# Two fp32 up projections between the spread and the dense stage, and the last 72 row fetches behind the scaling of zb

## The chip, the cores and the metric

One core of a Trainium2 chip runs the whole kernel. The metric is the device time of one execution in microseconds (us). The kernel before took 2037.93 us, the median of three runs (2034.81 to 2039.86). Engines are named as in the profile: PE (TensorE), DVE (VectorE), ACT (ScalarE), POOL (GpSimd) and SP (SyncE, which here only issues DMAs).

## The reference, cut to what matters

Two transformer blocks act on 512 tokens of width 1024, in float32. What the change touches is the end of the first block, a mixture of 16384 single-neuron experts, and the second block.

```python
# first block, per block of 128 tokens: 8 heads, 16 experts each, 128 in all per token
q = (xb @ wq).reshape(t, 8, 2, 128)
...                                   # two top-16 lists per head, joined to 16 experts
e = i1 * 128 + i2
g = softmax(c_top)
ue, ve = u[e], v[e]
act = gelu(einsum('thkd,td->thk', ue, xb))
x = x + einsum('thk,thkd->td', g * act, ve)
x = rmsnorm(x, final_norm_g)
# second block
h = rms_norm(x, g2)
q, k, v, qi, ki, wi, z_a, u_b, z_b, gates = split(h @ w_in_2)
a = dsa_attention(q, k, v, qi, ki, wi, 128) * silu(z_a)
b = multiscale_pool(u_b) * pool_scale * silu(z_b)
y = g0 * (a @ w_branch_a) + g1 * (b @ w_branch_b)
x = x + y @ w_out
```

## The kernel before, in words

The tokens form four tiles of 128, numbered 0 to 3. The experts are evaluated in two ways at once.

**Tiles 0 and 3 gather** (`gather`, L529). For each of the 128 experts k of a token, `fetch` (L552) has POOL issue an indirect DMA that brings one row of `peer_u` per token into a `rows` tile (128 x 1024, four buffers), and DVE multiplies and sums it with the token (L539). A second pass of 128 fetches brings rows of `peer_v`, and DVE adds each, scaled, to the accumulator `gx` (L546). So a tile needs 256 fetches, and each needs DVE before its buffer is free again. Constants `HOLDS = [168, 0]` say from which fetch on a tile waits for a mark, which is a small POOL copy near the end of the spread (`hold`, L610). All fetches of tile 3 wait for it.

**Tiles 1 and 2 are dense** (`first`, from L1016; `dense`, L620). All 16384 experts are computed for 256 tokens, in 128 groups e of 128 experts. An up projection `up(e)` (L595) loads 512 KB of `peer_u`, transposes it on PE (8 transposes), copies it out with ACT, multiplies it with the tokens, and applies Gelu. In the fp32 form (`xw` as the only operand) that is 16 matmul instructions and ACT copies; in the split form (`dh`, a high and a low fp32r half) it is 24, and DVE computes the low half of every transposed piece. Groups 0 to 36 (`EARLY`) and nine more (`WX`, kept in the pool `gb`) go through the fp32 form ahead of the dense loop. The **spread** (L559) writes the gates of all experts into `sa` and `sb` for four tokens at a time. After it, L1062 multiplies the nine kept results into `sb`, the pool `gb` is given up, `dh` is made from `xw` in its place (ACT, then DVE: L1065, by `split`, L129), and the **dense loop** starts: for each e a product with 512 KB of `peer_v` on PE (L646, half of the groups in three fp32r passes, the other half in fp32), and in between the up projections of groups 46 to 127 in the split form (L657).

**The second block** (`second`, L741) runs over the groups of tiles [0, 1, 2] and then [3]. For each group: add what the first block left (`after`, L661), two norms, transposes to `hl`, projections for qi/k/v, the index scores with 16 rounds of top-8 on DVE (`index`), projections for q, z_a, u_b and z_b (scaled on POOL at L821), attention (`attend`), the gates, the pooled branch, and two rounds of output projections. For three tiles every weight is split in two: ACT makes the high half, POOL the low one (L129, `wlo`). Tile 3 can't start before its last row has been added, and its `hl` lies in the buffer that the first group's last projection reads.

The program gives the order of the calls; a scheduler that simulates a timeline then fixes one order of instructions per engine, in which a later call can be moved ahead where its inputs are ready sooner. An engine works through its own list strictly in that order. `issue_after(mark)` keeps an instruction behind the marked one. The tile-3 gather is called at L1010, before the second block.

```python
for t, hold in zip(GATHER, HOLDS):
    n.gather(t, hold)
n.second_setup(b2)
for ts in GROUPS:
    n.second(ts, bp, bw)
```

Of the kernel before, what the change touches and what calls it, by code (L numbers as in the profile page):

```python
# [14 lines left out]
AF = mybir.ActivationFunctionType  # L15
OP = mybir.AluOpType
# [50 lines left out]
class Net:  # L67
# [197 lines left out]
    def mixer(self, ts):  # L265
# [17 lines left out]
        with tc.tile_pool(name="mq", bufs=1) as mq, tc.tile_pool(name="mw", bufs=2) as mw:  # L283
# [19 lines left out]
            def front(i, t, h):  # L303
                w_ = (t + 1) * P
                pe = []
                sm = mw.tile([P, 2], F32, name="sm", bufs=DEEP + 2)
                for p in range(2):
# [3 lines left out]
                    pe.append(self.expo(mw, s[:, :w_], self.abias[:, T - w_:T], w_, sm[:, p:p + 1], f"p{p}", slopes[h], P0B - p))  # L311
                r = mw.tile([P, 3], F32, name="rc", bufs=DEEP + 2)
                nc.vector.reciprocal(r[:, 0:2], sm)
# [214 lines left out]

    def gather(self, t, hold):  # L529

        nc, a = self.nc, self.a
        ei, gw = self.ei[t], self.gw[t]
        act = self.act[t]
        pause = self.normed if t == 0 else None
        xn = self.ga.tile([P, D], F32, name="gx", bufs=1)
        nc.sync.dma_start(xn, self.xnd[t])
        for k in range(P):
            r = self.fetch(a["peer_u"][0], ei, k, self.mark if k >= hold else pause if k >= PAUSE else None)
            nc.vector.scalar_tensor_tensor(r, r, 1.0, xn, op0=OP.mult, op1=OP.mult, accum_out=act[:, k:k + 1])  # L539
        nc.scalar.activation(act, act, AF.Gelu)  # L540
        nc.vector.tensor_tensor(act, act, gw, OP.mult)
        x = self.ga.tile([P, D], F32, name="gx", bufs=1)
        nc.sync.dma_start(x, self.xd[t])
        for k in range(P):
            r = self.fetch(a["peer_v"][0], ei, k, self.mark if P + k >= hold else pause)
            nc.vector.scalar_tensor_tensor(x, r, act[:, k:k + 1], x, op0=OP.mult, op1=OP.add)  # L546
        if t == GATHER[-1]:
            self.xs = {t: x}
        else:
            nc.sync.dma_start(self.xd[t], x)  # L550
# [44 lines left out]
    def up(self, e, hl, nt, dst, pool, half, bank=None):  # L595

        nc = self.nc
        u = self.st.tile([P, D], F32, name="raw", bufs=RAW)
        nc.sync.dma_start(u, self.a["peer_u"][0, e * P:(e + 1) * P, :])
        h = self.sc()  # L600
        for f in range(2):
            uT = [pool.tile([P, 4, P], x.dtype, name="uT", bufs=half) for x in hl]
            self.tsplit(uT, u[:, f * 512:(f + 1) * 512], 0, 0, bank)
            for k in range(4):
                ps = self.passes([x[:, k, :] for x in uT], [x[:, 4 * f + k, 0:nt] for x in hl])
                for q, (x, y) in enumerate(ps):
                    nc.tensor.matmul(h[:, :nt], x, y, start=f == k == q == 0, stop=f == 1 and k == 3 and q == len(ps) - 1)  # L607
        nc.scalar.activation(dst, h[:, :nt], AF.Gelu)  # L608

    def hold(self, gb):  # L610

        t = gb.tile([P, 1], F32, name="held")
        self.mark = self.nc.gpsimd.tensor_copy(t, self.sb_last).ins

    def early(self, e, hl, nt, wp, bufs, pool, half):
        w = wp.tile([P, nt], F32, name="w", bufs=bufs)
# [3 lines left out]
    def dense(self, ts, hl, sa, sb, dn, ue):  # L620

        nc, a = self.nc, self.a
        n = len(ts)
        nt = n * P
        mm = nc.tensor.matmul
        slot = lambda e: sa[:, e, :] if e < EARLY else sb[:, e - EARLY, :]

        V = {}

        def vp(e):  # L630
            V[e] = dn.tile([P, D], F32, name="v", bufs=VB)
            nc.sync.dma_start(V[e], a["peer_v"][0, e * P:(e + 1) * P, :])

        def op(e):
            v, w = [V.pop(e)], [slot(e)]
            if e % MIX[1] < MIX[0]:
                for x in (v, w):
                    hl_ = [dn.tile(list(x[0].shape), F32R, name=f"h{x[0].shape[1]}", bufs=1),
                           dn.tile(list(x[0].shape), F32R, name=f"l{x[0].shape[1]}", bufs=1)]
                    self.split(*hl_, x[0])  # L640
                    x[:] = hl_
            for i in range(n):
                for c in range(2):
                    ps = self.passes([x[:, i * P:(i + 1) * P] for x in w], [x[:, c * 512:(c + 1) * 512] for x in v])
                    for q, (x, y) in enumerate(ps):
                        mm(o[i][c], x, y, start=e == q == 0, stop=e == P - 1 and q == len(ps) - 1)  # L646

        o = [[self.acc() for _ in range(2)] for _ in range(n)]
        for e in range(VB - 1):
            vp(e)  # L650
        done = first = EARLY + WX
        for e in range(P):
            if e + VB - 1 < P:
                vp(e + VB - 1)
            op(e)
            while done < P and done - first < (e + 1) * (P - first) / LASTUP:
                nc.vector.tensor_tensor(slot(done), slot(done), self.early(done, hl, nt, dn, 1, ue, HALFE), OP.mult)  # L657
                done += 1
        self.sums = dict(zip(ts, o))
# [81 lines left out]
    def second(self, ts, bp, bw):  # L741

        nc, a = self.nc, self.a
        w = a["w_in_2"][0]
        n = len(ts)
        t0 = ts[0]
        ncol = n * P
        hl = self.pair(n)
        g_fin, g_2 = self.gains
        G = bp.tile([P, n, 2 * D], F32, name="G", padded_shape=[P, GN, 2 * D])  # L750
        for i, t in enumerate(ts):
            x = self.after(t)
            h = G[:, i, 0:D] if i else self.hn.tile([P, D], F32, name="h2", bufs=1)
# [9 lines left out]
        zb = bp.tile([P, n, 512], F32, name="zb", padded_shape=[P, GN, 512])  # L763
# [54 lines left out]

        def put_zb(i, p):
            nc.scalar.activation(zb[:, i, :], p, AF.Silu)  # L820
            nc.gpsimd.tensor_tensor(zb[:, i, :], zb[:, i, :], self.psc, OP.mult)  # L821

        self.proj(hl, w, 1064, 512, 8, n, put_za)
        nc.vector.tensor_copy(uT[:, :, 0:16], self.tail)
# [2 lines left out]
        self.proj(hl, w, 2088, 512, 8, n, put_zb)  # L827
        av = qk[:, :, 0:512]
        self.attend(ts, qT, bm, av, bw)
        for b in range(4):  # L830
            mb = self.row(bw, a["merge_bias_2"][0, b // 2, (b % 2) * 512:], 512, "once", bufs=OB, padded_shape=[P, 640])

            def put_g(i, p):
                d = G[:, i, b * 512:(b + 1) * 512]
                nc.vector.tensor_tensor(d, p, mb, OP.add)
                nc.scalar.activation(d, d, AF.Sigmoid)
            self.proj(hl, w, 2600 + b * 512, 512, 8, n, put_g)

        hl = self.pair(n)
# [25 lines left out]
        hl = self.pair(n)  # L865
# [101 lines left out]
RAW = 3  # L967
HALFE = 4
WX = 9
DEEP = 1  # L970
PEB = 2
P0B = 2
VB = 2
EARLY = 37
# [11 lines left out]
GATHER = [0, 3]  # L986
# [12 lines left out]
def build(tc, a, const_at, dbg=None):  # L999
    with ExitStack() as ctx:  # L1000
        n = Net(tc, ctx, a, const_at, dbg)
        pool = lambda name, bufs=1, **k: tc.tile_pool(name=name, bufs=bufs, **k)
        n.ga = ctx.enter_context(pool("ga", 2, side="right"))
        n.room(0, ctx.enter_context(pool("g0", side="right")))
        first(n, pool, ctx)
        n.tpn, n.nraw, n.whole, n.lone, n.lo_of = GN, 3, WHOLE, False, LO3
        with pool("tp2") as n.tp, pool("hn2", 2) as n.hn, pool("ws2") as n.ws, pool("b2") as b2, \
                pool("bp") as bp, pool("bw", 2) as bw:
            for t, hold in zip(GATHER, HOLDS):
                n.gather(t, hold)  # L1010
            n.second_setup(b2)
            for ts in GROUPS:
                n.second(ts, bp, bw)


def first(n, pool, ctx):  # L1016
    n.tpn, n.nraw = 3, 4
    n.whole, n.lone = WHOLE0, True
    nd = len(DENSE) * P
    with ExitStack() as right:  # L1020
# [27 lines left out]
        with pool("ue") as ue, pool("sa") as sap:  # L1048
            sa = sap.tile([P, EARLY, nd], F32, name="sa")
            for e in range(EARLY):  # L1050
                n.up(e, [n.xw], nd, sa[:, e, :], ue, HALFE, n.wide if e % 2 else None)
            for t in DENSE + [3]:
                n.select(t, se, idx, SP3 if t == 3 else 1)
            keys.close()
            with pool("sb") as sbp:
                sb = sbp.tile([P, P - EARLY, nd], F32, name="sb")
                with pool("gb", 2) as gb:
                    with n.tc.issue_after(n.picked):
                        ahead = [n.early(EARLY + i, [n.xw], nd, gb, WX, ue, HALFE) for i in range(WX)]
                    n.spread(idx, sa, sb, gb)  # L1060
                    for i, w in enumerate(ahead):
                        n.nc.vector.tensor_tensor(sb[:, i, :], sb[:, i, :], w, OP.mult)  # L1062
                with pool("dx") as dx:
                    dh = [dx.tile([P, 8, nd], F32R, name=f"dh{i}") for i in range(2)]
                    n.split(*dh, n.xw)  # L1065
                    picks.close()
                    with pool("dn", 2) as dn:
                        n.dense(DENSE, dh, sa, sb, dn, ue)
# [26 lines left out]
```

## Time and profile before

| what | us |
|---|---|
| median of three runs | 2037.93 (2034.81 to 2039.86) |
| the profiled execution | 2031.25 |
| its span in the profile | 2029.5 |
| PE busy | 1837.0 (91%) |
| DVE busy | 1515.5 (75%) |
| POOL busy | 859.6 (42%) |
| ACT busy | 741.0 (37%) |

The span is what the profiler sees of the execution, from the first instruction to the last; the 1.75 us that the profiled execution is longer lie around it. The shares are means over stages that have quite different limits, so they say little about a change in one place: at which time which engine idles, and for whom, is in the rows below.

### The profile page before, as it was taken

What the parts mean: (1) busy time and instruction counts of PE and PEld (TensorE: products, weight loads), DVE (VectorE), ACT (ScalarE), POOL (GpSimd) and SP (SyncE); (2) the same over time, 40 slices, a digit from 0 to 9 for tenths busy, and PEclk for the clock granted to TensorE, in tenths of its full rate; (3) what the DMA queues carried; (4) which work ended last, traced back from release to release, by engine and by line L of the source; (5) the groups of instructions that cost most, each with busy time, mean ns of one, the idle gap of its engine ahead of it and who ended that gap; (6) DMA issues with size and microseconds to landing.
All of it is one profiled execution on the core that took longest, in us unless ns stands there. A gap on an engine that the chain in (4) does not pass through costs nothing.

```text
span 2029.5 us, 27663 instructions
## 1 busy us (share of the span) xinstructions
PE 1837.0 (91%) x9646; PEld 1453.2 (72%) x9646; DVE 1515.5 (75%) x3064; ACT 741.0 (37%) x1504; POOL 859.6 (42%) x627
## 2 busy tenths in 40 slices
PE   7898988699989976999999999999976987889998
PEld 6597767699878965777877777777755765667644
DVE  1188998889995598877767777777878899974261
ACT  2243552333533784323232223232323333453231
POOL 0015566654344003454333444444448876654100
PEclk9999998799999998999999999999998897889999
DMA  9857998987566204999999999999988665762872
GB/s 342 280 167 255 314 323 290 326 293 252 175 208 236 88 22 179 358 353 344 367 328 343 347 356 345 345 352 336 359 275 301 220 192 177 234 200 80 304 258 83
DMA packets 182012, 538.23 MB, mean 265 GB/s; under 512 B 18032, under 2 KB 25328, under 8 KB 181744
## 3 DMA queue, kind: packets, MB, share of 16 engines
q1 hardware_dynamic: 108144, 268.00, 38.0%
q0 software_dynamic: 73728, 268.47, 37.2%
q8 instruction: 76, 1.25, 0.2%
q14 instruction: 64, 0.52, 0.1%
HBM read 528.53 MB, written 7.86 MB: 264 GB/s over the span
## 4 chain that ended last, share of the span: by engine, by line
PE 47%; DVE 18%; DMA 11%; issue 8%; POOL 3%; ACT 3%; SPq 0%; POOLq 0%; DVEq 0%; ACTq 0%
PE acc L646 17%; PE sc L607 13%; PE acc L205 9%; DMA rows<-in_peer_u,ei 4%; DMA rows<-in_peer_v,ei 4%; PE tr L154 4%; DVE gx L546 3%; POOL rows L555 3%; DVE rows L539 2%; ACT A L578 1%; DMA v<-in_peer_v 1%; PE acc L233 1%; DVE ix L406 1%; PE sc L927 1%; PE tr L936 1%
## 5 line engine op out<-in xcount | busy, mean ns | idle before, releaser
L555 POOL DMA_INDIRECT rows<-in_peer_u,ei x256 | 323.8, 1265 | 334.7 <-DVE rows L539 242.3
L555 POOL DMA_INDIRECT rows<-in_peer_v,ei x256 | 316.2, 1235 | 349.6 <-DVE gx L546 274.8
L546 DVE SCALAR_TENSOR_TENSOR gx<-rows,act,gx 128x1024 f32<-128x1024 f32 x256 | 384.5, 1502 | 47.9 <-DMA rows<-in_peer_v,ei 41.8
L539 DVE SCALAR_TENSOR_TENSOR rows<-rows,gx 128x1024 f32<-128x1024 f32 x256 | 310.8, 1231 | 37.8 <-DMA rows<-in_peer_u,ei 37.2
L607 PE MATMUL sc<-dh,uT 128*128 128x256 f32 x1968 | 296.4, 297 | 18.4 <-ACT dh L128 6.1
L607 PEld LDWEIGHTS sc<-dh,uT 128*128 128x128 f32 x1968 | 258.8, 191 | 54.0 <-issue 21.0
L205 PE MATMUL acc<-whi,Thi 128*128 128x512 f32 (+1 forms) x500 | 194.6, 427 | 25.5 <-ACT whi L128 17.8
L205 PE MATMUL acc<-wlo,Thi 128*128 128x512 f32 (+1 forms) x504 | 206.1, 428 | 9.7 <-POOL wlo L129 8.5
L607 PE MATMUL sc<-xw,uT 128*128 128x256 f32 x736 | 173.6, 387 | 14.4 <-ACT uT L157 14.3
L129 POOL TENSOR_TENSOR wlo<-raw,whi 128x1024 fp32r<-128x1024 f32 (+1 forms) x62 | 148.4, 2402 | 76.4 <-ACT whi L128 75.8
L205 PE MATMUL acc<-whi,Tlo 128*128 128x512 f32 (+1 forms) x432 | 171.4, 400 | 1.9 <-DVE Tlo L129 1.9
L646 PE MATMUL acc<-v,sb 128*128 128x512 f32 x368 | 165.7, 593 | 2.5 <-DMA v<-in_peer_v 2.4
L128 ACT ACTIVATE whi<-raw 128x1024 fp32r<-128x1024 f32 (+1 forms) x108 | 110.7, 1028 | 149.7 <-PE acc L205 67.8
L607 PEld LDWEIGHTS sc<-xw,uT 128*128 128x128 f32 x736 | 137.9, 194 | 32.8 <-ACT uT L157 15.8
L205 PEld LDWEIGHTS acc<-whi,Thi 128*128 128x128 f32 x500 | 97.7, 198 | 64.3 <-ACT whi L128 20.8
L129 DVE TENSOR_TENSOR uT<-tr,uT 128x512 fp32r<-128x512 f32 x164 | 109.0, 687 | 32.1 <-ACT uT L128 31.4
L205 PEld LDWEIGHTS acc<-wlo,Thi 128*128 128x128 f32 x504 | 100.4, 200 | 44.9 <-issue 15.6
L154 PE MATMUL tr<-c_ident,raw 128*128 128x128 f32 x880 | 130.6, 273 | 0.0
L128 ACT ACTIVATE uT<-tr 128x512 fp32r<-128x512 f32 x164 | 92.5, 595 | 81.1 <-PE tr L154 76.6
L608 ACT ACTIVATE w<-sc 128x256 f32<-128x256 f32 x91 | 34.8, 382 | 225.4 <-PE sc L607 220.6
L646 PEld LDWEIGHTS acc<-v,sb 128*128 128x128 f32 x368 | 66.4, 190 | 69.2 <-issue 66.1
L154 PEld LDWEIGHTS tr<-c_ident,raw 128*128 128x128 f32 x880 | 104.4, 141 | 10.9 <-issue 4.2
(332 smaller groups left out, 3362.6 us busy)
## 6 DMA issues: line engine op xcount, KB each, us to landing
raw<-in_peer_u SPq DMA_DIRECT2D x128, 512.0 KB, 6.4
v<-in_peer_v SPq DMA_DIRECT2D x128, 512.0 KB, 6.0
raw<-in_w_in SPq DMA_DIRECT2D x79, 512.0 KB, 4.7
raw<-in_w_out SPq DMA_DIRECT2D x22, 512.0 KB, 5.2
whi<-in_w_in SPq DMA_DIRECT2D x21, 512.0 KB, 6.5
raw<-in_peer_wq SPq DMA_DIRECT2D x21, 512.0 KB, 6.0
wlo<-in_w_in SPq DMA_DIRECT2D x20, 512.0 KB, 7.2
rows<-in_peer_u,ei POOLq DMA_INDIRECT x256, 6.9
```

The costliest lines, as they stand in the source:

```text
L128: self.nc.scalar.activation(hi, src, AF.Copy)
L129: (eng or self.nc.vector).tensor_tensor(lo, src, hi.bitcast(F32), OP.subtract)
L154: nc.tensor.transpose(p[:, c, :], src[:, (j + c) * P:(j + c + 1) * P], self.ident)
L205: self.nc.tensor.matmul(ps[i][:, :n], x, y, start=k == 0 and q == 0, stop=k == nk - 1 and q == len(ws) - 1)
L233: nc.tensor.matmul(ps[c][:, :ncol], x, y, start=k == 0 and q == 0, stop=k == 7 and q == len(ws) - 1)
L406: nc.vector.max_index(ix[:, r], v[:, r], src)
L539: nc.vector.scalar_tensor_tensor(r, r, 1.0, xn, op0=OP.mult, op1=OP.mult, accum_out=act[:, k:k + 1])
L546: nc.vector.scalar_tensor_tensor(x, r, act[:, k:k + 1], x, op0=OP.mult, op1=OP.add)
L555: self.nc.gpsimd.indirect_dma_start(out=r, out_offset=None, in_=src, in_offset=bass.IndirectOffsetOnAxis(ap=ei[:, k:k + 1], axis=0))
L607: nc.tensor.matmul(h[:, :nt], x, y, start=f == k == q == 0, stop=f == 1 and k == 3 and q == len(ps) - 1)
L608: nc.scalar.activation(dst, h[:, :nt], AF.Gelu)
L646: mm(o[i][c], x, y, start=e == q == 0, stop=e == P - 1 and q == len(ps) - 1)
```

## The change

The loop that starts the gathers now only runs each generator to its first `yield`. For tile 0 there is none and everything is issued as before. For tile 3 the generator stops ahead of fetch 56 of the `peer_v` pass; `second` resumes it after `attend` of the first group, and the 72 fetches left then wait for `scaled`, POOL's last multiplication of `zb` in that group, in place of the mark of the spread. Apart from that, groups 46 and 47 leave the dense loop: `link` computes their up projections in the fp32 form between the spread and the split of `xw`, leaves Gelu's result in PSUM, and DVE multiplies it into `sb` from there.

```diff
     def gather(self, t, hold):
...
         for k in range(P):
+            if t == GATHER[-1] and k == REST:
+                self.xs = {}
+                yield
+                hold, self.mark = 0, self.scaled
             r = self.fetch(a["peer_v"][0], ei, k, self.mark if P + k >= hold else pause)
...
-        nc.scalar.activation(dst, h[:, :nt], AF.Gelu)
+        h = h[:, :nt]
+        nc.scalar.activation(h if dst is None else dst, h, AF.Gelu)
+        return h
...
+    def link(self, e, hl, nt, dst, pool, half):
+
+        h = self.up(e, hl, nt, None, pool, half)
+        self.nc.vector.tensor_tensor(dst, dst, h, OP.mult)
...
-        done = first = EARLY + WX
+        done = first = EARLY + WX + LINK
...
-            nc.gpsimd.tensor_tensor(zb[:, i, :], zb[:, i, :], self.psc, OP.mult)
+            self.scaled = nc.gpsimd.tensor_tensor(zb[:, i, :], zb[:, i, :], self.psc, OP.mult).ins
...
         self.attend(ts, qT, bm, av, bw)
+        next(self.rest, None)
...
+LINK = 2
+REST = 56
...
-                n.gather(t, hold)
+                n.rest = n.gather(t, hold)
+                next(n.rest, None)
...
+                for e in range(EARLY + WX, EARLY + WX + LINK):
+                    n.link(e, [n.xw], nd, sb[:, e - EARLY, :], ue, HALFE)
                 with pool("dx") as dx:
```

## Rows read from the trace of the kernel before

**Rows 1.** The page, part 2: busy tenths in 40 slices of 50.7 us.

```profile
PE   7898988699989976999999999999976987889998
DVE  1188998889995598877767777777878899974261
```

**Rows 2.** Windows: stretch, length, busy time (instructions) per engine, clock, DMA share, GB/s.

```profile
710.00:780.00 70.00, 54.43 (x397) 47.23 (x395) 70.00 (x177) 63.00 (x199) 0.00 (x0) 1.00 0.05 16
780.00:793.00 13.00, 1.40 (x6) 0.93 (x5) 9.55 (x16) 2.33 (x2) 7.77 (x7) 0.69 0.58 202
793.00:1510.00 717.00, 707.00 (x3886) 545.07 (x3885) 547.62 (x766) 213.58 (x378) 316.69 (x260) 1.00 0.94 345
1530.00:1676.00 146.00, 122.07 (x562) 97.29 (x561) 132.25 (x167) 50.81 (x86) 116.58 (x75) 0.91 0.71 229
1676.00:1830.00 154.00, 124.04 (x525) 95.53 (x523) 135.65 (x221) 66.89 (x131) 94.04 (x60) 0.85 0.64 202
1830.00:1894.00 64.00, 60.44 (x292) 49.30 (x291) 23.12 (x33) 18.93 (x29) 24.49 (x10) 0.97 0.35 112
```

**Rows 3.** Timeline, spread to dense: start, us, engine, line, what [idle before <-releaser].

```profile
781.07 3.11 DVE L1062 TENSOR_TENSOR sb<-sb,w 128x256 f32<-128x256 f32 x9
...
784.30 1.91 ACT L128 ACTIVATE dh<-xw 128x2048 fp32r<-128x2048 f32 x1 [4.45 <-DVE sb L1062]
...
786.26 0.58 PE L607 MATMUL sc<-dh,uT 128*128 128x256 f32 x1 [6.08 <-ACT dh L128]
...
790.02 2.28 DVE L129 TENSOR_TENSOR dh<-xw,dh 128x2048 fp32r<-128x2048 f32 x1
...
792.36 4.48 PE L607 MATMUL sc<-dh,uT 128*128 128x256 f32 x25 [5.51 <-DVE dh L129]
```

**Rows 4.** Chain that ended last: one up projection's parts (start, us, what).

```profile
630.57 0.87 PE tr L154 x8
...
649.42 3.46 PE sc L607 x16
...
1203.66 2.86 PE sc L607 x24
```

**Rows 5.** Timeline of ACT in the spread: Gelu and a copy of transposes.

```profile
702.62 0.38 ACT L608 ACTIVATE w<-sc 128x256 f32<-128x256 f32 x1 [0.77 <-PE sc L607]
...
703.12 0.60 ACT L157 ACTIVATE uT<-tr 128x512 f32<-128x512 f32 x1
```

**Rows 6.** Windows of L546 alone: stretch, length, DVE busy (rows added), clock, DMA.

```profile
1383.00:1530.00 147.00, 66.68 (x52) 0.96 0.90 326
1530.00:1676.00 146.00, 67.81 (x37) 0.91 0.71 229
1676.00:1830.00 154.00, 77.17 (x39) 0.85 0.64 202
```

**Rows 7.** Chain that ended last, start of block 2.

```profile
1531.54 7.48 DMA rows<-in_peer_v,ei
...
1555.37 5.85 DVE gx L546
...
1566.87 7.78 DVE rope L717
```

**Rows 8.** Groups of instructions, 1676 to 1830: busy, mean ns | idle before <-releasers.

```profile
L129 POOL TENSOR_TENSOR wlo<-raw,whi 128x1024 fp32r<-128x1024 f32 x20 | 50.6, 2536 | 16.2 <-ACT whi L128 15.9
...
L555 POOL DMA_INDIRECT rows<-in_peer_v,ei x35 | 38.7, 1107 | 42.2 <-DVE gx L546 35.3 <-DVE asm L930 2.2 <-DVE isc L913 1.5
```

**Rows 9.** Timeline of POOL: the three multiplications of zb.

```profile
1675.93 3.73 POOL L821 TENSOR_TENSOR zb<-zb,psc 128x512 f32<-128x512 f32 x3
```

**Rows 10.** Timeline of DVE: the last row of tile 3 and its second norm.

```profile
1818.38 2.21 DVE L546 SCALAR_TENSOR_TENSOR gx<-rows,act,gx 128x1024 f32<-128x1024 f32 x1
...
1829.22 1.27 DVE L146 SCALAR_TENSOR_TENSOR h<-gx,rstd,norm_g 128x1024 f32<-128x1024 f32 x1
```

**Rows 11.** Chain that ended last: end of group [0, 1, 2], start of group [3].

```profile
1873.66 20.24 PE acc L205 x89
1893.92 0.61 ACT Thi L157
1894.57 12.86 PE acc L205 x44
```

## The prediction, made before the changed kernel was run

> **What bounds the kernel now.** I read the page's slices first, for the places where no engine is full [rows 1]: PE is at 7 and 6 in the two slices from 710 to 812 us and again in the two from 1471 to 1573, and mostly at 7 or 8 up to 1826. These are the two places that the change touches, so I cut windows there [rows 2]. In the spread (710 to 780) DVE is busy all the time and ACT for 63.0 of 70 us, while PE has 15.6 us free. From 780 to 793 PE works for only 1.40 of 13 us. The dense stage (793 to 1510) is PE's: 707 of 717 us. In block 2 no engine is full for long: from 1530 to 1676 PE idles 146 - 122 = 24 us, from 1676 to 1830 it idles 30 us, from 1830 to 1894 only 3.6 us; DVE is busy 132 of 146 and 136 of 154 us in the first two.
>
> The timeline shows the first hole: DVE multiplies nine kept results until 784.2, ACT then makes the high half of `dh`, and DVE makes the low half only at 790.02, though ACT was done at 786.2; PE idles 6.08 and 5.51 us for the two halves [rows 3]. The chain shows what fills the front of block 2: landings of rows, products of rows, and a tiny rope operation of 7.78 us [rows 7]. Block 2's second group starts at 1893.9, when the first group's last projection is done [rows 11]; tile 3 had its norm ready at 1830.5 [rows 10]. So tile 3's rows have 63 us of slack today, and the first group sets the end.
>
> **The links.** Removed from the dense loop: two split up projections, each 24 matmuls (2.86 us) and eight transposes (0.87 us) [rows 4], so 2 x 3.73 = 7.5 us of a stage in which PE hardly idles. Added: two fp32 ones, 16 matmuls (3.46 us) and the same transposes, 2 x 4.33 = 8.7 us of PE. They need only `xw` and weights that are loaded early, so they can run in the 15.6 us that PE has free in the spread or in the 11.6 us after it [rows 2, 3]; without that cover they would cost all 8.7. ACT has for each two copies of 0.60 and a Gelu of 0.38 [rows 5], 3.2 us for both, in the 7 us that it has free; DVE gains two products, at 3.11 / 9 = 0.35 us each [rows 3], 0.7 us ahead of `dh`, and loses the low halves of the transposed pieces. The new wait, of these products for Gelu, has `dh`'s low half and tile 3's queued row products behind it on DVE. SP issues the same loads. I take 1 us for the seam: **-6.5 us**. Bounds: -7.5 if all is hidden, +2 if the links run after the spread and `dh` waits for them (780.2 + 8.7 = 788.9 in place of 786.2, less the 0.7 that two products fewer give in the loop).
>
> **The rows that leave the front.** From 1383 to 1530 52 rows are added [rows 6], so fetch 56 comes about 1540. Of the 37 rows from 1530 to 1676, 33 move away, at 67.81 / 37 = 1.83 us each: 60 us of DVE's 132. The fetches go as well, and with them the waits in POOL's list ahead of the splits of weights, for which PE waits. PE's own work is then the limit: at most its 24 us of idle time can go. I take two thirds, 16 us, since projections still wait in turn for rope, norms and rounds of index scores on DVE: **-16 us**. Bounds 0 and -24. POOL's last scaling of `zb` ends at 1679.7 [rows 9]; it moves to 1679.7 - 6.5 - 16 = 1657.
>
> **The rows behind it.** The mark is an instruction of POOL itself, so nothing waits on it but the fetches; behind a fetch that waits for a buffer stand splits of weights (20 in 154 us, 2.54 us each), and POOL already waits 42 us there [rows 8]. Now 72 rows follow the scaling, not 39. Their spacing is not shown for this mix. The nearest rows bound it: 147 / 52 = 2.83 us in the dense stage, and (1820.6 - 1676) / 39 = 3.71 us in this very stretch [rows 6, 10], where DVE had the rounds of index scores as well. I take 2.83: much of that other work moves ahead of the mark into the time that the 33 rows leave, and after it DVE is mostly free (23 of 64 us busy from 1830 to 1894 [rows 2]). Rows end at 1657 + 72 x 2.83 = 1861; norm and transposes take 11 us more (1820.6 to 1830.5 [rows 10], and a copy), 1872. The first group's own end, unchanged in length behind the scaling, comes at 1657 + (1893.9 - 1679.7) = 1871. Both agree: group [3] starts at about 1872, not 1893.9. The stage behind it is left as it is.
>
> **Sum: -22 us** (-6.5 - 16, and 0 for the tail). Against the profiled execution that is 2031 - 22 = 2009; the median of the runs lies 6.7 us above that execution, so I expect **2016 us**.
>
> **A rule against it.** In the dense stage a row's product takes 66.68 / 52 = 1.28 us; in the last stretch, beside POOL's splits, 77.17 / 39 = 1.98 us [rows 6]. The Trainium skill (SBUF — State Buffer, section "SBUF: two separate sides") says that DVE, with two inputs from SBUF, and GpSimd, reading SBUF, take one port pair in turn, and the loser waits for the other's whole instruction. By that rule, if every row met a split, 72 rows would take up to 72 x (1.28 + 2.54) = 275 us, and the sum would be +49 in place of -22. The trace agrees that there is such a cost, with 0.70 us a row as its mean; the third rival takes its full weight.
>
> **The rivals.**
> - *More is won.* The front loses all 24 us of PE's idle time and the tail a third of its 30: -6.5 - 24 - 10 = -40, 1998 us. For it: DVE's share of row work there is that large. Against it: rows must then come every 2.7 us or faster (1649 to 1843). Chance 0.17.
> - *Only the links count.* DVE's dependent rounds and POOL's splits, not the rows, set the front, or what the front wins is given back waiting for tile 3: -6.5, 2031 us. For it: POOL idles 16 us for ACT's high halves in the tail, so weights have their own chain [rows 8]. Against it: rows stand in the chain itself [rows 7]. Chance 0.20.
> - *Slower: the last rows gate group [3].* Each fetched row meets POOL's splits and DVE's other work as it does today in that stretch, one per 3.71 us: 1657 + 267 + 11 = 1935, 41 us after today's start: 2079 us. It decides from (1893.9 - 11 - 1657) / 72 = 3.14 us a row. For it: that spacing is measured in the same stage. Against it: DVE's other work there gets less, and the last 40 us of the tail leave it free. Chance 0.13.
> - *The links don't go into the hole.* They stand where they are written, and `dh` comes late: +2 in place of -6.5, so -13.5, 2024 us. Chance 0.08.
> - *As forecast*: chance 0.42.
>
> **How the numbers follow.** A measurement of this kernel tells about 0.3% (6 us) from no change. The forecast, the first and the fourth rival are faster, and half of the second, which lies on the edge: 0.42 + 0.17 + 0.08 + 0.10 = 0.77. The same: 0.10. Slower: 0.13. The range goes from 1994 (past the first rival's 1998) to 2042 (past the second's 2031, and with rows at 3.2 us, a little above the point of no gain); it leaves out most of the slower rival and the far end of the first.
>
> **What would show it.** Right: PE's free time from 780 to 793 gets no larger and the loop holds 80 up projections; `zb` is scaled some 22 us earlier; between about 1535 and 1657 there is no row; the last row comes at about 1860, every 2.8 us; the second group starts at about 1872, with PE waiting neither for it nor much before. Wrong: `zb` scaled less than 10 us earlier; a gap on PE ahead of the second group while tile 3's rows are still coming; links behind `dh`.

## The result, and the profile after

The changed kernel took 2015.34 us, the median of four runs (2009.53 to 2021.84), beside 2038.08 us before; the measured ratio is 0.9898 with a 95% interval of 0.987 to 0.9925, or -20.8 us (the two medians alone differ by 22.7). The forecast was 2016 us (-22). A second measurement further down gave 0.9926 (0.9901 to 0.9952). So the sum came out; two of its three terms did not. The profiled execution took 2013.95 us, its span is 2012.2.

The page's slices of the kernel after, to be read against [rows 1]:

```profile
PE   7898998799989996999999999999996989897798
DVE  1188988888996598877767777777877699887371
```

The dip of PE at the start of block 2 (7 and 6 in two slices before) is down to one slice, and a new low, 7 and 7, stands in slices 37 and 38, near 1860 us. The windows of the kernel after (columns as in [rows 2]) show both:

```profile
1537.00:1645.00 108.00, 105.14 (x517) 82.36 (x515) 81.55 (x182) 49.57 (x87) 67.02 (x36) 1.00 0.43 126
1645.00:1800.00 155.00, 131.26 (x590) 101.21 (x590) 140.40 (x186) 64.93 (x131) 117.61 (x75) 0.90 0.77 251
1800.00:1858.00 58.00, 49.43 (x209) 39.41 (x208) 49.14 (x38) 13.02 (x15) 47.70 (x29) 0.91 0.81 265
1858.00:1876.00 18.00, 2.40 (x12) 1.77 (x11) 8.01 (x10) 2.90 (x5) 1.44 (x3) 0.58 0.73 269
```

From 1537 to 1645 PE works 105 of 108 us at full clock, where the like stretch before had 122 of 146 at 0.91 [rows 2]. From 1858 to 1876 it does nearly nothing, at a clock of 0.58 (mostly the lower of the two levels, 1.2 of 2.4 GHz, after PE had run out of work at 1858.5). The waits of PE, from 1535 to 1880, name the reason (for whom: us, times, longest):

```profile
PE tr L154 <- DVE h L146: 15.6, 1, 15.6
PE sc L940 <- DVE mx L373: 9.5, 4, 7.2
PE tr L949 <- ACT aT L383: 6.1, 1, 6.1
```

`h` at L146 is the second norm of tile 3: PE waits for its last rows. These lines of the timelines of POOL and DVE answer to [rows 9, 10]:

```profile
1640.63 4.53 POOL L833 TENSOR_TENSOR zb<-zb,psc 128x512 f32<-128x512 f32 x3 [5.57 <-ACT zb L832]
...
1862.96 3.91 DVE L551 SCALAR_TENSOR_TENSOR gx<-rows,act,gx 128x1024 f32<-128x1024 f32 x3
...
1872.63 1.28 DVE L146 SCALAR_TENSOR_TENSOR h<-gx,rstd,norm_g 128x1024 f32<-128x1024 f32 x1 [0.68 <-POOL rstd L137]
```

And these are PE's transposes of tile 3, and the first copy of them by ACT:

```profile
1874.06 1.94 PE L154 MATMUL tr<-c_ident,h 128*128 128x128 f32 x8 [15.60 <-DVE h L146]
1875.18 0.60 ACT L157 ACTIVATE Thi<-tr 128x512 f32<-128x512 f32 x1 [3.73 <-PE tr L154]
```

So `zb` is scaled by 1645.2, the last row is added at 1866.9, and group [3] has its first transposed copy at 1875.2, not 1893.9.

The seam between spread and dense loop, the timelines of ACT, DVE and PE, against [rows 3]:

```profile
720.40 0.37 ACT L614 ACTIVATE sc<-sc 128x256 f32<-128x256 f32 x1
...
730.24 0.36 ACT L614 ACTIVATE sc<-sc 128x256 f32<-128x256 f32 x1
...
783.36 3.10 DVE L1078 TENSOR_TENSOR sb<-sb,w 128x256 f32<-128x256 f32 x9
...
786.38 0.74 DVE L625 TENSOR_TENSOR sb<-sb,sc 128x256 f32<-128x256 f32 x2
...
792.37 2.28 DVE L129 TENSOR_TENSOR dh<-xw,dh 128x2048 fp32r<-128x2048 f32 x1
...
794.71 5.30 PE L612 MATMUL sc<-dh,uT 128*128 128x256 f32 x25 [5.59 <-DVE dh L129]
```

Both links are done inside the spread: their Gelus, PSUM onto itself, run at 720 and 730 us, and only DVE's two products, 0.74 us, wait for the end. The hole behind the spread is as wide as it was.

To compare executions, I cut each timeline at three events: the end of the dense loop's last product, the end of the scaling of `zb`, and the start of the first transposed copy of group [3]. "Front" is from the first to the second, "tail" from the second to the third. Behind the third all kernels take 136 to 140 us. The start of the dense loop itself lies between 791.7 and 799.2 us, in no order that follows the edits, so lengths are compared, not times. The orders of the engines' lists differ a little from kernel to kernel, so the cut at the scaling does not part the same work in each: the front holds 573 matmul instructions before and in the changed kernel, but 553 with 56 rows and 559 with the fetches only. Front and tail together don't depend on that cut.

| kernel | dense loop ends | `zb` scaled | front | group [3] starts | tail |
|---|---|---|---|---|---|
| before | 1514.2 | 1679.7 | 165.5 | 1893.9 | 214.2 |
| changed | 1510.7 | 1645.2 | 134.5 | 1875.2 | 230.0 |
| changed, again | 1513.3 | 1649.7 | 136.4 | 1876.8 | 227.1 |
| links only | 1508.2 | 1675.0 | 166.8 | 1894.0 | 219.0 |
| rows only | 1523.9 | 1663.7 | 139.8 | 1894.8 | 231.1 |
| 66 rows behind | 1511.9 | 1655.3 | 143.4 | 1863.3 | 208.0 |
| 66 rows, again | 1511.7 | 1659.0 | 147.3 | 1866.4 | 207.4 |
| 56 rows behind | 1506.3 | 1655.0 | 148.7 | 1881.9 | 226.9 |
| 72 rows dropped | 1513.3 | 1651.1 | 137.8 | 1823.2 | 172.1 |
| fetches only | 1509.6 | 1656.1 | 146.5 | 1850.0 | 193.9 |
| products only | 1511.4 | 1671.8 | 160.4 | 1882.9 | 211.1 |
| no mark | 1514.8 | 1679.5 | 164.7 | 1891.3 | 211.8 |
| 66 rows, split work shared | 1517.4 | 1661.5 | 144.1 | 1864.9 | 203.4 |

### The profile page after: what moved, and what is told of

Same layout as the page of the kernel before. It is cut to its first block, busy times and chain, and to the rows that moved or that the text cites. A ratio compares the mean times of both kernels' runs of the same rounds, so it can differ in the third digit from the quotient of the medians.

```text
span 2012.2 us, 27611 instructions
## 1 busy us (share of the span) xinstructions
PE 1830.0 (91%) x9630; PEld 1445.9 (72%) x9630; DVE 1505.7 (75%) x3060; ACT 735.5 (37%) x1502; POOL 851.4 (42%) x627
## 4 chain that ended last, share of the span: by engine, by line
PE 56%; DVE 16%; DMA 12%; issue 8%; POOL 5%; ACT 2%; SPq 0%; POOLq 0%; DVEq 0%; ACTq 0%
PE acc L658 17%; PE sc L612 13%; PE acc L205 10%; PE acc L233 6%; DMA rows<-in_peer_u,ei 5%; PE tr L154 4%; DMA rows<-in_peer_v,ei 4%; POOL rows L560 3%; DVE gx L551 2%; DVE rows L540 2%; POOL wlo L129 2%; DMA v<-in_peer_v 1%; PE acc L585 1%; DVE ix L406 1%; DVE v L404 1%
## 5 line engine op out<-in xcount | busy, mean ns | idle before, releaser
L560 POOL DMA_INDIRECT rows<-in_peer_u,ei x256 | 318.2, 1243 | 342.7 <-DVE rows L540 255.5
L551 DVE SCALAR_TENSOR_TENSOR gx<-rows,act,gx 128x1024 f32<-128x1024 f32 x256 | 383.8, 1499 | 50.7 <-DMA rows<-in_peer_v,ei 43.2
L612 PE MATMUL sc<-dh,uT 128*128 128x256 f32 x1920 | 288.3, 297 | 18.3 <-ACT dh L128 6.1
L612 PEld LDWEIGHTS sc<-dh,uT 128*128 128x128 f32 x1920 | 251.5, 192 | 50.4 <-issue 19.4
L612 PE MATMUL sc<-xw,uT 128*128 128x256 f32 x768 | 181.5, 386 | 14.2 <-ACT uT L157 14.1
L612 PEld LDWEIGHTS sc<-xw,uT 128*128 128x128 f32 x768 | 143.5, 194 | 33.2 <-ACT uT L157 15.7
L128 ACT ACTIVATE whi<-raw 128x1024 fp32r<-128x1024 f32 (+1 forms) x108 | 110.8, 1028 | 136.4 <-PE acc L205 64.6
```

The costliest lines, as they stand in the source:

```text
L128: self.nc.scalar.activation(hi, src, AF.Copy)
L560: self.nc.gpsimd.indirect_dma_start(out=r, out_offset=None, in_=src, in_offset=bass.IndirectOffsetOnAxis(ap=ei[:, k:k + 1], axis=0))
```

## The experiments

**The two parts, each alone.**

```diff
-REST = 56
+REST = 999
```

> Only the links; the gather of tile 3 is issued as before. The dense loop ended 3.5 us earlier in the changed kernel's profile (1514.2 to 1510.7), less than the 6.5 us of the prediction. If the links are worth what that profile shows, the time is 2034.5 us; if they are worth the predicted term, 2031.5 us. If they win nothing and all comes from the rows: 2038 us.

Measured: 2032.21 us, ratio 0.9972 (0.9957 to 0.9987), -5.7 us. Front and tail are no shorter than before (166.8 and 219.0 us), so the gain lies ahead of them, and the predicted -6.5 is well inside the interval. The profiles show where: from the first matmul behind `dh`'s low half to its last product, the dense loop takes 721.8 and 724.7 us in the two kernels without links, and 710.5 to 718.8 us, 715.7 on average, in the eleven profiles with them. That is 7.6 us less; 7.5 was forecast for the work removed.

```diff
-LINK = 2
+LINK = 0
```

> Only the 72 rows behind the scaling of zb; groups 46 and 47 stay in the dense loop. If the two parts add up, the time is 2015 + 3.5 = about 2019 us (with the links worth 6.5: 2022 us). If the rows are worth nothing without the links, it is near 2035 us.

Measured: 2030.67 us, ratio 0.9962 (0.9947 to 0.9976), -7.7 us: less than either expectation for a sum. The front falls to 139.8 us and the tail grows to 231.1, as in the changed kernel. The parts add to -13.4 us, the changed kernel had -20.8, so it was run again beside others, with no edit:

> The changed kernel once more, beside the others of this call. The links alone gave 0.9972 and the rows alone 0.9962, which add to -13.4 us; the changed kernel was measured at 0.9898, -20.8 us. If the parts only add up, this run comes near 0.9935 (2025 us); if each needs the other, it stays near 0.990 (2017 us).

Measured: 2017.72 us, ratio 0.9926 (0.9901 to 0.9952), -15 us. The two measurements of the changed kernel average to about -18; with intervals of some 5 us on each and 3 us on each part, no need of one part for the other is shown, and none is excluded.

**How many rows to leave behind.**

```diff
-REST = 56
+REST = 62
```

> The changed kernel with 66 rows behind the scaling, not 72. Theory one, tile 3's last rows gate group [3] (PE waits 15.6 us for its norm): at 3.08 us a row the last row comes 18 us earlier, the wait closes, and the front pays 6 rows x 0.94 us (31 us won there for 33 rows): about -10, 2005 us. Theory two, the first group's own end sets the start of group [3] and the wait is beside the point: only the front's 6 us are paid, 2021 us.

Measured: 2009.49 us, ratio 0.986 (0.9834 to 0.9885). The front pays 9 us for the six rows and the tail gives back 22, the way of theory one. The windows of front and tail of this kernel, columns as in [rows 2]:

```profile
1511.90:1655.30 143.40, 117.78 (x572) 93.66 (x573) 117.23 (x216) 58.36 (x102) 96.96 (x59) 0.90 0.53 171
1655.30:1863.30 208.00, 177.70 (x803) 138.70 (x804) 189.78 (x223) 80.40 (x150) 159.85 (x99) 0.92 0.78 259
```

DVE is busy 190 of 208 us in the tail. Tile 3's norm is ready at 1861.3 us, while PE is still in the first group's last projection; it goes from there to tile 3's transposes without a wait:

```profile
1862.45 0.40 PE L205 MATMUL acc<-whi,Tlo 128*128 128x512 f32 x1
1862.68 1.04 PE L154 MATMUL tr<-c_ident,h 128*128 128x128 f32 x8
```

So with 66 rows tile 3 no longer gates group [3]: the 15.6 us of waiting are gone. The other 6 us come from the first group, whose last projection ends 207.5 us behind the scaling and not 213.3 as with 72 rows; theory one did not have that part. The same kernel once more, beside two others further down:

> The kernel with 66 rows behind the scaling once more, since 72 and 56 rows both came out slower than 66 did. If the best lies there, 0.984 to 0.988 again; if the first run of it was a lucky chip, it comes near the 0.990 to 0.993 of the changed kernel.

Measured: 2015.19 us, ratio 0.9901 (0.9881 to 0.992), above the first range that was expected and just inside the second; but both runs were on one chip, so a lucky chip does not explain the first. Front 147.3, tail 207.4. The two measurements average to 0.988, against 0.991 for the two of the changed kernel. That the tail is 20 us shorter is seen twice; by the time of the whole, the better count is likely, not certain.

```diff
-REST = 56
+REST = 72
```

> 56 rows behind the scaling of zb, not 72 (nor the 66 of the run before, 0.986). If a row in the tail costs 3.1 us while tile 3's rows gate group [3], and 0.94 us in the front, the gate opens at about 66 rows; from there on fewer rows in the tail only lengthen the front, 10 rows x 0.94 us: about 2018 us, 0.990. If the first group's own tail also shortens with fewer rows beside it, as without any of them (172 us in place of 230), it wins on: about 2000 us, 0.982.

Measured: 2025.64 us, ratio 0.9964 (0.9944 to 0.9983). Both expectations fail. The rows do end early (1841.7 us, norm at 1850.0), so they don't gate; but group [3] waits until 1881.9 for the first group. The waits of PE in this tail, 1655 to 1885:

```profile
PE sc L940 <- DVE mx L373: 13.0, 4, 7.9
PE tr L154 <- DVE G L876: 8.3, 1, 8.3
PE tr L154 <- DVE Tlo L129: 7.6, 1, 7.6
```

These are pieces of the first group's own work on DVE. The last two stand behind row products in DVE's list; ahead of the wait of 8.3 us a single row product takes 8.45 us, from 1829.6. The longest wait for the attention's maxima, until 1664.7, stands behind rounds of index scores and the pooled branch, with no row product there. The order of the lists differs from count to count (this tail holds 825 matmuls, that of the changed kernel 803), so one step of the count can win or lose more than its rows.

**The tail without rows.** The last 72 rows of tile 3 are neither fetched nor added; the output of tile 3 lacks them.

```diff
+            if t == GATHER[-1] and k >= REST:
+                continue
             r = self.fetch(a["peer_v"][0], ei, k, self.mark if P + k >= hold else pause)
```

> The changed kernel without the last 72 rows of tile 3: neither fetched nor added. It shows what the first group does with no rows beside it. If rows hold the tail up, PE's own 181 us of busy time from 1645 on set its length: group [3] starts about 1830, 1970 us in all. If the splits of weights and DVE's rounds set the tail, the first group ends near 1857 as in the changed kernel: about 1998 us. The front, where no row stood in the changed kernel either, should end at 1645 in both.

Measured: 1962.32 us in one run. Windows of front and tail:

```profile
1513.30:1651.10 137.80, 116.83 (x573) 92.77 (x572) 110.94 (x209) 60.46 (x106) 91.01 (x55) 0.93 0.50 158
1651.10:1823.20 172.10, 167.98 (x805) 132.60 (x804) 66.09 (x156) 83.75 (x151) 72.08 (x30) 0.99 0.34 110
```

With no rows the tail is PE's: 168 of 172 us busy at a clock of 0.99. The front is about what it is in the changed kernel; in both, 13 products of earlier rows of tile 3 still stand in it, so it was not free of rows as the expectation had it. So the 72 rows cost 230 - 172 = 58 us where they are now, and the first group's own work allows a tail of 172 us, not of 214 as my sum assumed.

**Which half of a row holds the front.** The rows of tile 3 are put back where they were before; of the last 72 only the fetch is left in one kernel, and only the product (each time with the row of fetch 55) in the other. Both leave out the rest of those rows' work.

```diff
+            if t == GATHER[-1] and k >= PART:
+                continue
             nc.vector.scalar_tensor_tensor(x, r, act[:, k:k + 1], x, op0=OP.mult, op1=OP.add)
```

> The links as in the changed kernel, and the rows in the front as before, but of tile 3's last 72 rows only the fetch, not the product: DVE loses 72 x 1.28 us, POOL and the transfers keep theirs. From the end of the dense loop to the scaling of zb it was 165.5 us before and 134.5 in the changed kernel. If the products hold DVE, and with it the front: near 137 us. If it is the fetches in POOL's list ahead of the splits of weights, and the transfers: 155 to 166 us.

Measured: 1991.06 us in one run, front 146.5 us.

```diff
+            if t != GATHER[-1] or k < PART:
-            r = self.fetch(a["peer_v"][0], ei, k, self.mark if P + k >= hold else pause)
+                r = self.fetch(a["peer_v"][0], ei, k, self.mark if P + k >= hold else pause)
```

> The counterpart: 72 products on DVE, all with the row that fetch 55 brought, and no fetch for them. The same stretch: near 165 us if the products hold the front, 137 to 145 us if the fetches do. A product then waits for no landing, so many can run inside the dense loop; if so the front shows fewer than 33 of them, and its length counts per product that is left there.

Measured: 2022.29 us in one run, front 160.4 us. The groups of the two fronts (line, engine, operation, count, busy us, mean ns), fetches only first:

```profile
L562 POOL DMA_INDIRECT rows<-in_peer_v,ei x45 | 51.9, 1153 | 14.6 <-issue 9.0 <-DVE ms L135 4.3 <-DVE Tlo L129 0.3
L553 DVE SCALAR_TENSOR_TENSOR gx<-rows,act,gx 128x1024 f32<-128x1024 f32 x14 | 20.4, 1461 | 4.0 <-DMA rows<-in_peer_v,ei 3.9
```

```profile
L552 DVE SCALAR_TENSOR_TENSOR gx<-rows,act,gx 128x1024 f32<-128x1024 f32 x55 | 92.7, 1685 | 3.8 <-DMA rows<-in_peer_v,ei 3.5
...
L561 POOL DMA_INDIRECT rows<-in_peer_v,ei x11 | 15.7, 1423 | 7.0 <-DVE ms L135 4.9 <-issue 1.8 <-DVE Tlo L129 0.3
```

Against 134.5 to 137.8 us with 9 fetches and 13 products in the front, 45 fetches lengthen it by about 10 us, 55 products by about 24, and both together (43 rows, before) by about 30. The products did not move into the dense loop: 55 stand in the front, not fewer than 33. So the two fronts carry different doses. Front and tail together carry nearly the same in each kernel (83 fetches; 87 products): 309.9 us with neither, 340.4 with the fetches only, 371.5 with the products only, 385.8 with both (links only). That is 31, 62 and 76 us: the products on DVE are the larger part, the fetches are not free. These are single runs, and in the fetch-only kernel no fetch waits for a product to free its buffer, so that wait is in neither half. My sum had counted on both without saying which.

**The mark itself.**

```diff
-                hold, self.mark = 0, self.scaled
+                hold = 2 * P
```

> The changed kernel, with the 72 fetches still called behind attention, but with no mark to wait for. If the place in the program alone keeps them out of the front, nothing changes: 0.990. If the scheduler moves them ahead into the front's free time on POOL, the front gets longer again, up to its 165 us, and the tail shorter: between 0.990 and the 0.997 of the links alone.

Measured: 2032.95 us, ratio 0.998 (0.9963 to 0.9996). The scheduler puts 43 products back into the front, which is 164.7 us long again. The place of the call is worth nothing; the wait does it.

**What spaces the rows in the tail.** On top of 66 rows, half of the splits behind the first group's attention go to DVE.

```diff
         next(self.rest, None)
+        self.lo_of = (1, 2)
         for b in range(4):
```

> 66 rows behind the scaling of zb, and in the first group, behind attention, every second low half of a weight made by DVE and not by POOL. In the tail of the changed kernel POOL goes through two fetches and one split in turn, a row each 3.08 us. If POOL's list sets that spacing, 15 splits of 2.5 us less bring the last row 15 to 35 us earlier, and group [3] starts with the first group's end: 10 us or so below the run with 66 rows (0.986), about 0.981. If DVE sets it, 15 splits at 1.2 us more on DVE make the last row about 18 us later: about 0.995.

Measured: 2008.11 us, ratio 0.9863 (0.9843 to 0.9882); the kernel with 66 rows, measured beside it, had 0.9901 (0.9881 to 0.992). Neither expectation holds. The groups of the two tails, shared splits first:

```profile
L551 DVE SCALAR_TENSOR_TENSOR gx<-rows,act,gx 128x1024 f32<-128x1024 f32 x66 | 106.2, 1610 | 6.6 <-DMA rows<-in_peer_v,ei 4.1 <-issue 2.2
L129 POOL TENSOR_TENSOR wlo<-raw,whi 128x1024 fp32r<-128x1024 f32 x15 | 37.4, 2494 | 3.2 <-issue 3.0
L560 POOL DMA_INDIRECT rows<-in_peer_v,ei x66 | 77.6, 1176 | 72.0 <-DVE gx L551 57.5 <-DVE asm L944 4.7 <-issue 4.1
L129 DVE TENSOR_TENSOR wlo<-raw,whi 128x1024 fp32r<-128x1024 f32 x14 | 20.8, 1483 | 0.5 <-ACT whi L128 0.5
```

```profile
L551 DVE SCALAR_TENSOR_TENSOR gx<-rows,act,gx 128x1024 f32<-128x1024 f32 x66 | 131.3, 1990 | 7.9 <-DMA rows<-in_peer_v,ei 7.1
L129 POOL TENSOR_TENSOR wlo<-raw,whi 128x1024 fp32r<-128x1024 f32 x30 | 74.9, 2501 | 3.8 <-ACT whi L128 3.3
L560 POOL DMA_INDIRECT rows<-in_peer_v,ei x66 | 83.8, 1269 | 37.7 <-DVE gx L551 24.6 <-issue 9.1 <-DVE mx L373 1.4
```

Half of the splits gone from POOL, a product falls from 1.99 to 1.61 us: DVE gains 25 us on the products and spends 21 on the splits, so it is nearly as full as it was (181 of 203 us, before 189 of 207), while POOL loses 37 us. The last row comes (1852.1 - 1661.5) = 190.6 us behind the scaling, before it was 197.9. So each engine's share of the spacing is partly the other's: POOL's list alone doesn't set it, and DVE's isn't independent of it. DVE is the fuller of the two, and POOL's idle time ahead of fetches, most of it for DVE's products, grows from 37.7 to 72.0 us. An earlier last row could not have won anything by itself, since with 66 rows tile 3 no longer gates group [3]; the tail is 4 us shorter because the first group's own end comes earlier. This is the fastest kernel beside the first run with 66 rows; its lead of 0.4% over the one beside it is at the edge of the intervals.

## Why the prediction was right, and where it was not

**The links: right.** -6.5 us was forecast, the run with the links alone shows -5.7 (1.3 to 4.3 parts in a thousand). The loop is 7.6 us shorter, where the sum took out 7.5; the 1 us for the seam is too small to be seen. The cover is the spread's, as the sum allowed; the fourth rival, links behind the spread, is out: PE had them done at about 730 us. The hole from 782 to 795 stayed.

**The front: right in kind, half of its size.** The step "at most its 24 us of idle time can go. I take two thirds, 16 us" failed. In the profiles the front fell by 165.5 - 134.5 = 31 us. The windows of the whole front, before and after, columns as in [rows 2]:

```profile
1514.20:1679.70 165.50, 126.47 (x573) 100.91 (x573) 149.25 (x183) 55.48 (x94) 128.93 (x88) 0.88 0.73 238
1510.70:1645.20 134.50, 117.55 (x573) 93.28 (x573) 103.40 (x205) 58.31 (x102) 87.97 (x52) 0.92 0.52 155
```

Two things were wrong with the bound. Of the 24 us of idle time nearly all went, not two thirds: PE idles 39.0 us in the whole front before and 17.0 after, and some 19 of these 22 us lie in the window that I took. And I took PE's busy time as work that stays: for the same 573 matmul instructions it fell by 8.9 us, from 126.5 to 117.6, with the mean granted clock at 0.88 before and 0.92 after. By the clocks alone it would have come to 126.5 x 0.88 / 0.92 = 121 us, an estimate, so they account for some 5 us of it; the rest is not explained. That products on DVE do more of it than fetches, which the text left open, the runs with half rows show. In time, the 16 us for the rows came out as 7.7 when the rows were moved alone, and as 9 to 15 beside the links (15.0 to 20.8, less the links' 5.7).

**The tail: the failed term on the other side.** "I take 2.83" us a row came out as (1866.9 - 1645.2) / 72 = 3.08, and "the first group's own end" came at 1858.5, 15.6 us before PE could go on with tile 3. So the third rival's mechanism, tile 3's rows gating group [3], is what happens, and with it one of the prediction's own signs of being wrong: a gap on PE ahead of the second group while tile 3's rows are still coming. Its price is 15.8 us (230.0 against 214.2) and not 41, since the spacing is nearer to the dense stage's than to the old tail's. My tail term of zero held only because a scaling forecast 12 us too late and rows forecast 0.25 us too fast cancel in the start of group [3]: 1872 forecast, 1875.2 seen. The sum was right by two errors of about 15 us each, of opposite sign, and that is luck. "Unchanged in length" held for the first group beside the rows (213.3 us from the scaling to its last projection's end, against 214.2), but it was no law of the program: without rows its tail takes 172 us.

**The rule on the shared port.** It was weighed as an upper bound, every row meeting a split. A product took 1.28 us in the dense stage [rows 6] and takes 1.91 in the new tail, so the loss is 0.63 a row, a quarter of a split, about what the old tail's 0.70 said. The Trainium skill (SBUF — State Buffer, section "SBUF: two separate sides") has the two engines take one port pair in turn; the runs agree from both sides: products get faster when splits leave POOL (1.99 to 1.61 us), and splits take 2.75 us on average in the tail with 32 products that need no fetch, 2.41 in the tail with none (2.50 in the changed kernel). The mean hides that one product either pays or doesn't: in the changed tail 50 of the 72 products took 1.26 to 1.29 us, as in the dense stage, and 22 took 2.28 to 5.99 us. So most products met no split at all, which is why the bound was far from the mean.

**What stays open.** Whether POOL's list or DVE's would set the rows' pace if the other were free; whether 66 rows is the best count, since the order of every engine's list changes with it; and why two measurements of one kernel lie 0.3 to 0.4% apart (those with 66 rows on the same chip), which is the size of what the last steps are worth. A fifth row buffer was not run.

## What to carry to other kernels

Work that only has to be done by some later time should be held back by an explicit wait until the critical stage is over: called later but free to move, it went straight back. Then look for the new end of the line: hold back only as much as still finishes when the other work does, and bound a gain not by an engine's idle time alone but by what the stage takes with the rival work taken out. A sum that hits the total can hide two wrong terms, so compare the lengths of the stages, not the end.

## What was not expected of the hardware

The same 573 matmul instructions of the front were busy for 126.5 us before and 117.6 after, at mean granted clocks of 0.88 and 0.92. The records show two levels, 2.4 and 1.2 GHz, so these means are about a quarter and a sixth of the stretch at the lower one. Without rows the tail ran at 0.99, with 72 of them at 0.88.

A DVE operation could last through several of POOL's splits in a row, not only one. A row product takes 1.28 us alone, and a rope operation on 128x36 elements 0.19 us at its neighbours in the same timeline. Here are a rope operation before (the chain of [rows 7] has it with 7.78 us) and a row product in the kernel with 56 rows, each with POOL's splits at that time:

```profile
1566.79 7.86 DVE L717 TENSOR_TENSOR rope<-qi,sin 128x36 f32<-128x36 f32 x1
1567.40 2.37 POOL L129 TENSOR_TENSOR wlo<-raw,whi 128x1024 fp32r<-128x1024 f32 x1
1569.97 4.62 POOL L129 TENSOR_TENSOR wlo<-raw,whi 128x1024 fp32r<-128x1024 f32 x2
...
1829.59 8.45 DVE gx L551
1829.92 7.02 POOL L129 TENSOR_TENSOR wlo<-raw,whi 128x1024 fp32r<-128x1024 f32 x3
```

The rope operation ends at 1574.65 with the third split (1574.59); the row product ends 1.1 us behind the third split (1836.94).
